# The first group of a feed-forward layer as plain products, and the block forms of x for two pairs at once

## The chip, the core and the metric

One core of a Trainium2 chip runs the whole program. The time is that of one execution on the device, in microseconds; the median of several runs is given. The engines run side by side, each with its own queue in program order: TensorE (PE), VectorE (DVE), ScalarE (ACT), GpSimd (POOL), and SyncE (SP), which issues most transfers. POOL issues the transfers that add to what lies in SBUF already.

## The reference

One layer on 512 tokens with 1024 features, in float32. The change touches the first line inside the loop:

```python
h = h + 0.5 * swiglu(rmsnorm(h, ffn1_norm[i]), ffn1_w_gate[i], ffn1_w_up[i], ffn1_w_down[i])
...
h = h + 0.5 * swiglu(rmsnorm(h, ffn2_norm[i]), ffn2_w_gate[i], ffn2_w_up[i], ffn2_w_down[i])
gate = jax.nn.sigmoid(rmsnorm(h, ple_norm[i]) @ ple_w_gate[i] + ple_b_gate[i])
h = h + gate * (p[i] @ ple_w_proj[i])
...
def swiglu(x, w_gate, w_up, w_down):
    return (jax.nn.silu(x @ w_gate) * (x @ w_up)) @ w_down
```

The hidden width of a feed-forward is 2816. Between the two stand a token mixer and its projections, which the change leaves alone.

## The kernel before

Features lie on the 128 partitions, tokens along the free side: `h[0..7]` are eight tiles of 128 x 512. Every product is done in three passes of a short format: an operand is split into a high part (a cast, ScalarE) and a low part (the difference, VectorE), and the passes are high by high, high by low and low by high (`whi`, `wlo` for weights; `Parts.split`, L422 and L423). The gain of the norm is applied to x first, the factor per token only behind the product, so the products need not wait for the norm.

A feed-forward works in 11 groups of 256 hidden columns. For a group, gate and up together are a 2 x 2 block product: the rows of blocks are up and gate, the inner blocks are the lower and upper four feature tiles, and the columns are the first and second 256 tokens. `Group` computes the four results with seven block products in place of eight (numbers 1 to 7), from sums of weight blocks and from block forms of x. With X11, X12 the two token halves of a tile of the first four and X21, X22 those of its partner four tiles on (a pair), the forms are X11, X2 (both halves), T3 = X22 - X12, T2 = X11 - T3, T4 = X21 - T2 and T1 = X11 - X12. They lie split in `xfa` and `xfb`, one of each per pair. Weight sums are made by accumulating transfers of POOL (L594, L606, L645) and by one addition on VectorE (L589). A block product is 24 matmuls with 256 columns (four pairs, two column blocks, three passes). `mm`, `acc` and `sm` are the tags of eight PSUM banks. Product 1 goes to an `mm` bank; `seed` copies it into an `acc` bank (L665), which products 6, 5 and 3 add to, while product 2 adds to the `mm` bank itself. A matmul of no use opens the `acc` bank in the first two groups (L653). `keep_p7` and `keep_u2` copy other partial results out.

The norm of the first feed-forward is formed beside the products: ScalarE squares the tiles of h, VectorE adds the squares (`ssum`, L266), TensorE sums them over partitions (L275), VectorE forms the inverse root, TensorE spreads it to all partitions (L305), ScalarE keeps it (`rall`, L311). Only then can gates be scaled and put through Silu.

The program starts with the embedding: two steps of 24 matmuls of 512 columns (L214 to L216), whose results ScalarE copies out (L832) and POOL stores to DRAM (L792). Then come, in the first feed-forward, products of group 0 and of group 1 mixed: (0,1), (1,1), (0,2), (0,7), (0,6), (1,2), (0,5), (0,4), (0,3), where (group, product) names a step; then (1,7), (1,6), (1,4), (1,5), (1,3) with two steps of the down projection between them. `run` writes all engines' queues from this list: the split of a step's weights stands two steps ahead of its product, its loads six, its `after` work one or two behind, and `also` and `ahead` hang further work on a step's split. Queues are strictly in that order. Split weights rotate through three buffers, a second pair (`whix`, `wlox`) serves steps that are named so.

In the first feed-forward, the block forms are made by `XForms.all_of` from h itself, scaled by the gain as they are split:

```python
also(steps[1], "split", blocks("X11", "X12"))
ahead(steps[3], "split", blocks("X2"))
ahead(steps[4], "split", blocks(("T3", 0)))
```

In the second one, `first` and `second` form them tile by tile as h becomes ready.

## Time and profile before

| | us |
|---|---|
| median of 3 runs (lowest, highest) | 1132.74 (1131.59, 1134.9) |
| the profiled execution | 1130.95 |
| its span, first to last instruction | 1129.2 |
| TensorE busy | 1085.7 (96%) |
| VectorE busy | 800.6 (71%) |
| ScalarE busy | 503.4 (45%) |

Mean granted TensorE clock 0.989. A row of the timeline reads: start, duration, engine, source line, operation, written tile <- read tiles, shape, count, and in brackets how long the engine had been idle and what ended that. A row of the chain has start, length, engine, tile, line. A row of a stretch has its bounds and length, then busy time and count of PE, PEld (weight loads), VectorE, ScalarE, POOL, and the granted clock, the share of the DMA engines and GB/s. Matmuls overlap in their records, so the pace is read from start to start and not from a duration.

### The profile page before, as it was taken

What the parts mean: (1) busy time and instruction counts of PE and PEld (TensorE: products, weight loads), DVE (VectorE), ACT (ScalarE), POOL (GpSimd) and SP (SyncE); (2) the same over time, 40 slices, a digit from 0 to 9 for tenths busy, and PEclk for the clock granted to TensorE, in tenths of its full rate; (3) what the DMA queues carried; (4) which work ended last, traced back from release to release, by engine and by line L of the source; (5) the groups of instructions that cost most, each with busy time, mean ns of one, the idle gap of its engine ahead of it and who ended that gap; (6) DMA issues with size and microseconds to landing.
All of it is one profiled execution on the core that took longest, in us unless ns stands there. A gap on an engine that the chain in (4) does not pass through costs nothing.

```text
span 1129.2 us, 16802 instructions
## 1 busy us (share of the span) xinstructions
PE 1085.7 (96%) x6781; PEld 963.6 (85%) x6781; DVE 800.6 (71%) x1099; ACT 503.4 (45%) x671; POOL 177.1 (16%) x161
## 2 busy tenths in 40 slices
PE   9589999999999999999999999998999999999997
PEld 7488999999998788777778888887999999999887
DVE  5767766766776687799875565767876676767766
ACT  6544444344344365423543343534444344344554
POOL 2000000000000301476421100010100000000312
PEclk9799999999999999999999999999999999999999
DMA  9667756666733222354333233588766667553412
GB/s 358 148 171 190 223 144 177 169 178 186 195 94 103 72 85 90 96 175 122 112 93 94 75 93 114 148 201 208 191 186 184 174 163 189 155 141 96 148 57 75
DMA packets 50190, 165.87 MB, mean 147 GB/s; under 512 B 5697, under 2 KB 5953, under 8 KB 50113
## 3 DMA queue, kind: packets, MB, share of 16 engines
q1 hardware_dynamic: 34416, 118.50, 30.9%
q0 software_dynamic: 10096, 36.70, 18.3%
q10 hardware_dynamic: 5600, 9.60, 2.8%
q8 instruction: 53, 0.87, 0.3%
q14 instruction: 25, 0.20, 0.1%
HBM read 160.52 MB, written 4.26 MB: 146 GB/s over the span
## 4 chain that ended last, share of the span: by engine, by line
PE 75%; DVE 11%; DMA 5%; ACT 4%; issue 3%; POOL 2%; DVEq 0%; ACTq 0%; POOLq 0%
PE mm L579 17%; PE acc L579 13%; PE sm L215 7%; PE sm L216 7%; PE sm L214 7%; PE mm L214 4%; PE mm L216 4%; PE mm L215 4%; PE acc L214 3%; PE acc L216 3%; PE acc L215 3%; DMA s<-in_ffn_gu 2%; DVE wlo L423 1%; ACT whi L422 1%; DMA u<-cs_dram 1%
## 5 line engine op out<-in xcount | busy, mean ns | idle before, releaser
L579 PE MATMUL mm<-xfb,whi 128*128 128x256 f32 x992 | 175.8, 280 | 12.4 <-ACT p L669 5.9
L579 PEld LDWEIGHTS mm<-xfb,whi 128*128 128x128 f32 x992 | 153.4, 191 | 15.2 <-ACT p L669 6.3
L423 DVE TENSOR_TENSOR wlo<-raw,whi 128x1024 fp32r<-128x1024 f32 x95 | 116.3, 1225 | 70.2 <-ACT whi L422 68.9
L422 ACT CAST whi<-raw 128x1024 fp32r<-128x1024 f32 x95 | 99.3, 1046 | 97.9 <-issue 38.9
L579 PE MATMUL mm<-xfb,wlo 128*128 128x256 f32 x496 | 138.8, 280 | 1.4 <-DVE wlo L423 1.4
L579 PE MATMUL acc<-xfb,whi 128*128 128x256 f32 x704 | 122.5, 276 | 1.8 <-ACT whi L422 1.1
L216 PE MATMUL sm<-ghi,wlox 128*128 128x512 f32 x296 | 116.5, 393 | 1.2 <-DVE wlox L423 1.2
L214 PE MATMUL sm<-ghi,whix 128*128 128x512 f32 x296 | 115.4, 390 | 0.7 <-ACT whix L422 0.7
L215 PE MATMUL sm<-glo,whix 128*128 128x512 f32 x296 | 115.9, 391 | 0.0
L579 PEld LDWEIGHTS acc<-xfb,whi 128*128 128x128 f32 x704 | 107.5, 188 | 3.9 <-ACT whi L422 1.2
L579 PE MATMUL acc<-xfb,wlo 128*128 128x256 f32 x352 | 97.5, 277 | 2.2 <-DVE wlo L423 2.2
L579 PEld LDWEIGHTS mm<-xfb,wlo 128*128 128x128 f32 x496 | 94.5, 190 | 2.1 <-DVE wlo L423 2.1
L423 DVE TENSOR_TENSOR wlox<-rawd,whix 128x1024 fp32r<-128x1024 f32 (+1 forms) x40 | 45.7, 1142 | 57.4 <-ACT whix L422 57.4
L689 ACT ACTIVATE g<-g 128x512 f32<-128x512 f32 x44 | 27.8, 632 | 121.0 <-DVE g L688 121.0
L594 POOL DMA_DIRECT2D raw<-in_ffn_gu x22 | 18.9, 858 | 389.4 <-DVE h L742 158.8
L184 ACT CAST whi<-raw 128x1024 fp32r<-128x1024 f32 x44 | 45.8, 1044 | 61.1 <-PE mm L215 22.7
L423 DVE TENSOR_TENSOR wlo<-rawb,whi 128x1024 fp32r<-128x1024 f32 x48 | 58.7, 1223 | 19.3 <-ACT whi L422 19.3
L742 DVE SCALAR_TENSOR_TENSOR h<-sm,h 128x512 f32<-128x512 f32 x96 | 63.4, 685 | 10.8 <-PE sm L216 10.2
L185 DVE TENSOR_TENSOR wlo<-raw,whi 128x1024 fp32r<-128x1024 f32 x44 | 57.5, 1308 | 18.9 <-ACT whi L184 13.8
L579 PEld LDWEIGHTS acc<-xfb,wlo 128*128 128x128 f32 x352 | 66.1, 188 | 2.8 <-DVE wlo L423 2.8
L216 PEld LDWEIGHTS sm<-ghi,wlox 128*128 128x128 f32 x296 | 55.5, 188 | 13.7 <-DVE wlox L423 2.1
L214 PEld LDWEIGHTS sm<-ghi,whix 128*128 128x128 f32 x296 | 55.6, 188 | 11.8 <-ACT whix L422 1.1
(366 smaller groups left out, 2644.9 us busy)
## 6 DMA issues: line engine op xcount, KB each, us to landing
raw<-in_ffn_gu SPq DMA_DIRECT2D x56, 512.0 KB, 5.9
rawd<-in_ffn_down SPq DMA_DIRECT2D x40, 512.0 KB, 4.1
raw<-in_ffn_gu POOLq DMA_DIRECT2D x34, 512.0 KB, 5.6
rawb<-in_ffn_gu SPq DMA_DIRECT2D x32, 512.0 KB, 5.4
raw<-in_w_in SPq DMA_DIRECT2D x29, 512.0 KB, 3.6
s<-in_ffn_gu SPq DMA_DIRECT2D x22, 512.0 KB, 7.1
s<-in_ffn_gu POOLq DMA_DIRECT2D x22, 512.0 KB, 8.5
raw<-in_w_out SPq DMA_DIRECT2D x16, 512.0 KB, 3.7
```

What stands on the lines that cost most here:

```text
L184: nc.scalar.copy(self.hi[:, c], self.raw[:, c])
L185: nc.vector.tensor_tensor(self.lo[:, c], self.raw[:, c], self.hi[:, c].bitcast(F32), ALU.subtract)
L214: nc.tensor.matmul(ps, whi, xhi, start=first, stop=False)
L215: nc.tensor.matmul(ps, whi, xlo, start=False, stop=False)
L216: nc.tensor.matmul(ps, wlo, xhi, start=False, stop=last)
L422: nc.scalar.copy(self.hi[:, :n], raw[:, :n])
L423: nc.vector.tensor_tensor(self.lo[:, :n], raw[:, :n], self.hi[:, :n].bitcast(F32), ALU.subtract)
L579: nc.tensor.matmul(o, wt[:, c], xt, start=fresh and p == m == n == 0, stop=last and n == 2, skip_group_check=True,)
L594: nc.gpsimd.dma_start(w21.raw, self.src[0], accum_op=ALU.add)
L689: nc.scalar.activation(t, t, AF.Silu)
L742: nc.vector.scalar_tensor_tensor(h[d], ps[d], 0.5, h[d], ALU.mult, ALU.add)
```

## The change

Group 0 of the first feed-forward is no longer seven block products but four plain steps: gate with the first four feature tiles, up with them, then gate and up with the other four. Each step is two chains, one per 128 output columns, of 12 matmuls with all 512 tokens: eight chains of 512 tokens in all. They need only X11, X12, X21 and X22, and the four weight blocks as they are, without sums. Group 1 follows whole, as (1,1), (1,7), (1,2), (1,6), (1,4), (1,5), (1,3). Its forms come from a copy of h that ScalarE scales by the gain once (`Early.x`), and each form is made for two pairs in one instruction (`Early.t`); `xfa` and `xfb` now hold two pairs each. The squares stand with the splits of steps 4 and 5 in place of 6 and 7, ahead of T3, T2, T4 and T1. The sums for the norm follow the second plain step, and the spread uses their bank. `plain_gate` scales and gates group 0 as soon as the norm is kept, `plain_finish` multiplies by up. One padding of 480 bytes goes. The second feed-forward keeps its steps.

```diff
-    "D1": 1, "X12": 1, "F": 1, "xfa": 4, "xfb": 4, "x": 16, "xs": 8, "u": 8, "emb": 8, "raw0": 1, "embt": 1, "rawb": 3,
+    "D1": 1, "X12": 1, "F": 1, "xfa": 2, "xfb": 2, "x": 16, "xs": 8, "u": 8, "emb": 8, "raw0": 1, "embt": 1, "rawb": 3,
-PAD = {"sb": 480, "ffn_left": 96, "mix_left": 160, "ple_left": 160, "ffn_right": 0, "mix_right": 96, "ple_right": 0}
+PAD = {"sb": 0, "ffn_left": 96, "mix_left": 160, "ple_left": 160, "ffn_right": 0, "mix_right": 96, "ple_right": 0}
-        def spread(diag):
-            ps = sm_ps()
+        def spread(diag, ps=None):
+            ps = sm_ps() if ps is None else ps
             nc.tensor.matmul(ps, ones, diag, start=True, stop=True)
-                got["ps"] = self.spread(got["diags"])
+                got["ps"] = self.spread(got["diags"], got["ps"])
+        def __init__(self, xfs):
+            if len(xfs) % 2:
+                self.both_a, self.both_b = xfs[-1].both_a, xfs[-1].both_b
+            else:
+                self.both_a = sb("xfa", (P, 2, 2, 2, HT), F32R)
+                self.both_b = sb("xfb", (P, 5, 2, 2, HT), F32R)
+            self.a, self.b = (t[:, :, :, len(xfs) % 2] for t in (self.both_a, self.both_b))
+            xfs.append(self)
-        @staticmethod
-        def all_of(xfs, what, stage=None):
...
+    class Early:
+        def __init__(self, a, b, d, name):
+            self.a, self.b, self.d, self.name = a, b, d, name
+            self.hg = [None, None]
+        def x(self, lower):
+            self.hg[lower] = sb(("ghi", "glo")[lower], (P, 2, T))
+            to = (self.a, self.b)[lower][:, 0:2]
+            for k in range(2):
+                d = self.d + k + NP * lower
+                nc.scalar.activation(self.hg[lower][:, k], h[d], AF.Copy, scale=col(self.name, d))
+            t = self.hg[lower].rearrange("p k (s t) -> p s k t", s=2)
+            nc.scalar.copy(to[:, :, 0], t)
+            nc.vector.tensor_tensor(to[:, :, 1], t, to[:, :, 0].bitcast(F32), ALU.subtract)
+        def t(self, i):
+            x11, x12, x21, x22 = (
+                t.rearrange("p k (s t) -> p s k t", s=2)[:, s] for t in self.hg for s in range(2)
+            )
+            if i == 3:
+                self.f = sb(("ghi", "glo")[self.d // 2], (P, 2, 2, HT))
+            n = (3, 2, 4, 1).index(i) % 2
+            f, other = self.f[:, n], self.f[:, 1 - n]
+            if i in (3, 1):
+                nc.vector.tensor_tensor(f, *((x22, x12) if i == 3 else (x11, x12)), ALU.subtract)
+            else:
+                nc.vector.scalar_tensor_tensor(
+                    f, x11 if i == 2 else x21, -1.0, other, ALU.mult, ALU.subtract
+                )
+            to = self.a[:, 1] if i == 1 else self.b[:, {3: 2, 2: 3, 4: 4}[i]]
+            nc.scalar.copy(to[:, 0], f)
+            nc.vector.tensor_tensor(to[:, 1], f, to[:, 0].bitcast(F32), ALU.subtract)
-            self.first, self.leads, self.last = j < 2, j == 0, j == sum(G_PARTS) - 1
-
-            self.other_pair = (1, 2, 7) if j == 1 else ()
+            self.first = j in ((1, 2) if plain else (0, 1))
+            self.early = j == 1 if plain else j < 2
+            self.leads, self.last = j == 0, j == sum(G_PARTS) - 1
+            self.other_pair = (1, 2, 7) if j == 1 and not plain else ()
-            early = self.first
+            early = self.early
+        def plain_steps(self):
+            self.g = sb("g", (P, 2, 2, HT))
+            self.ps = {}
+            def step(w, i, which, lower):
+                w_parts = {}
+                def split():
+                    w_parts[0] = w.split()
+                def product():
+                    whi, wlo = w_parts[0]
+                    if not lower:
+                        self.ps[which] = (
+                            [sm_ps(), sm_ps()] if which == "gate" else [bank("mm", 3), bank("acc", 2)]
+                        )
+                    for m, ps in enumerate(self.ps[which]):
+                        for p, xf in enumerate(self.xfs):
+                            c = slice((2 * p + m) * P, (2 * p + m + 1) * P)
+                            t = (xf.a, xf.b)[lower]
+                            passes(
+                                by_half(ps), whi[:, c], wlo[:, c], t[:, 0:2, 0], t[:, 0:2, 1],
+                                not lower and p == 0, lower and p == len(self.xfs) - 1,
+                            )
+                return Step(product, lambda: self.load((w, i)), None, split)
+            return [
+                step(*s) for s in (
+                    (self.w21, 2, "gate", False), (self.w11, 0, "up", False), (self.w22, 3, "gate", True), (self.w12, 1, "up", True),
+                )
+            ]
+        def plain_gate(self):
+            for m, ps in enumerate(self.ps["gate"]):
+                t = self.g[:, :, m]
+                nc.vector.tensor_tensor(t, by_half(ps), by_half(self.shared["r"]), ALU.mult)
+                nc.scalar.activation(t, t, AF.Silu)
+        def plain_finish(self):
+            for m, ps in enumerate(self.ps["up"]):
+                t = self.g[:, :, m]
+                nc.vector.tensor_tensor(t, t, by_half(self.shared["r"]), ALU.mult)
+                nc.vector.tensor_tensor(t, t, by_half(ps), ALU.mult)
-            if half == 0 or self.hi is None:
+            if half or self.last:
+                self.parts_of_g(slice(half, half + 1) if self.last else slice(0, 2))
+        def parts_of_g(self, part):
+            if self.hi is None:
                 self.hi = sb("ghi", (P, 2, 2, HT), F32R)
                 self.lo = sb("glo", (P, 2, 2, HT), F32R)
-            if half == 0 and not self.last:
-                return
-            part = slice(half, half + 1) if self.last else slice(0, 2)
-    def swiglu(name, xfs, norm, closed, after, at=2):
+    def swiglu(name, xfs, norm, closed, after, plain):
-        groups = [Group(src[j], xfs, shared, j) for j in range(sum(G_PARTS))]
-        gs = [g.steps() for g in groups]
+        groups = [Group(src[j], xfs, shared, j, plain) for j in range(sum(G_PARTS))]
+        gs = [None if plain and g.leads else g.steps() for g in groups]
-        steps = [gs[j][i] for j, i in ((0, 1), (1, 1), (0, 2), (0, 7), (0, 6), (1, 2), (0, 5), (0, 4), (0, 3))]
+        if plain:
+            steps = groups[0].plain_steps()
+        else:
+            steps = [gs[j][i] for j, i in ((0, 1), (1, 1), (0, 2), (0, 7), (0, 6), (1, 2), (0, 5), (0, 4), (0, 3))]
-                    for i in (7, 6, 4, 5, 3) if j == 1 else (1, 7, 6, 4, 5, 2, 3):
+                    for i in ((1, 7, 2, 6, 4, 5, 3) if plain else (7, 6, 4, 5, 3)) if j == 1 else (1, 7, 6, 4, 5, 2, 3):
-        norm.behind(steps[at:], D, lambda r: shared.update(r=r))
+        def use(r):
+            shared.update(r=r)
+            if plain:
+                groups[0].plain_gate()
+        norm.behind(steps[0 if plain else 2 :], D, use)
+        if plain:
+            also(gs[1][1], "after", groups[0].plain_finish)
+            also(gs[1][7], "after", lambda: groups[0].parts_of_g(slice(0, 2)))
-                ps.append(bank("mm", 3) if q == 0 and i < 3 else sm_ps() if i else bank("acc", 2))
+                ps.append(bank("acc", 2) if i == 3 else bank("mm", 3) if q else sm_ps())
-        splitter("mix_norm", x_mix), 3,
+        splitter("mix_norm", x_mix), True,
+        XForms(x_ffn1)
+    early = [Early(x_ffn1[d].both_a, x_ffn1[d].both_b, d, "ffn1_norm") for d in (0, 2)]
-    also(steps[2], "load", lambda: load_x(4, 5, 6, 7))
-
-    also(steps[1], "split", blocks("X11", "X12"))
-    ahead(steps[3], "split", blocks("X2"))
-    ahead(steps[4], "split", blocks(("T3", 0)))
-    ahead(steps[5], "split", blocks(("T3", 1)))
-    ahead(steps[6], "split", blocks(("T2", 0)))
-    also(steps[6], "split", blocks(("T2", 1)))
-    also(steps[7], "split", blocks("T1"))
-    also(steps[8], "split", blocks("T4"))
-    for k in range(2):
-        also(steps[6 + k], "split", lambda k=k: [norm.add(h[d]) for d in range(4 * k, 4 * k + 4)])
-    also(steps[6], "split", store_embedding)
+    also(steps[3], "load", lambda: load_x(4, 5, 6, 7))
+    also(steps[1], "split", lambda: [e.x(0) for e in early])
+    also(steps[3], "split", lambda: [e.x(1) for e in early])
+    also(steps[4], "split", lambda: squares(0, 1, 2, 3))
+    also(steps[5], "split", lambda: squares(4, 5, 6, 7))
+    also(steps[4], "split", store_embedding)
+    for k, i in enumerate((3, 2, 4, 1)):
+        also(steps[6 + k], "split", lambda i=i: [e.t(i) for e in early])
```

TensorE's queue at the sums for the norm, before (`acc_263` is product 6 of group 0, `mm_307` product 2 of group 1):

```order
L579 MATMUL acc_263<-xfb_250,whi_375 128x256 x2
L579 MATMUL acc_263<-xfb_250,wlo_376 128x256
L275 MATMUL sm_491<-ones_78,ssum_388 128x1 x4
L579 MATMUL mm_307<-xfb_247,whix_437 128x256 x2
L579 MATMUL mm_307<-xfb_247,wlox_438 128x256
```

And now (`acc_311` is up with the first four tiles, `sm_257` gate, which the other four tiles add to):

```order
L215 MATMUL acc_311<-xfa_113,whi_241 128x512
L216 MATMUL acc_311<-xfa_113,whi_241 128x512
L217 MATMUL acc_311<-xfa_113,wlo_242 128x512
L276 MATMUL sm_352<-ones_78,ssum_294 128x1 x4
L215 MATMUL sm_257<-xfb_112,whi_290 128x512
```

The sums moved from behind five products of 256 columns to behind two plain steps, ahead of the other two.

ScalarE's queue around a seed, before (`acc_263<-mm_265` is the seed of group 0, `acc_305<-mm_307` that of group 1):

```order
L422 CAST whi_301<-rawb_133 128x1024
L665 COPY acc_263<-mm_265 128x512
L504 CAST xfb_247<-ghi_166 128x256
L504 CAST xfb_248<-glo_168 128x256
L504 CAST xfb_249<-ghi_170 128x256
L504 CAST xfb_250<-glo_172 128x256
L422 CAST whi_341<-raw_135 128x1024
L665 COPY acc_305<-mm_307 128x512
```

And now around the seed of group 1 (`acc_447<-mm_449`; the casts into `xfb` from `ghi_385` and `glo_389` are T4, `g_109` the gates of group 0, `whi_523` the weights of product 6):

```order
L423 CAST whi_474<-rawb_255 128x1024
L527 CAST xfb_112<-ghi_385 128x512
L527 CAST xfb_114<-glo_389 128x512
L312 COPY rall_485<-sm_352 128x512
L712 ACT_TABLE_LOAD
L712 ACTIVATE g_109<-g_109 128x2x256 x2
L721 COPY acc_447<-mm_449 128x512
L423 CAST whi_523<-rawb_165 128x1024
```

The seed has moved behind T4, the kept norm, the load of the Silu table and both gates of group 0.

VectorE's queue, before, where T2 is formed and split behind product 6's weights and the additions of squares follow:

```order
L589 TENSOR_TENSOR raw_23_125<-raw_23_125,s_41_174 128x1024
L497 SCALAR_TENSOR_TENSOR ghi_166<-h_101,negffn_norm_111,ghi_166 128x256
L497 SCALAR_TENSOR_TENSOR glo_168<-h_102,negffn_norm_111,glo_168 128x256
L497 SCALAR_TENSOR_TENSOR ghi_170<-h_103,negffn_norm_111,ghi_170 128x256
L497 SCALAR_TENSOR_TENSOR glo_172<-h_104,negffn_norm_111,glo_172 128x256
L423 TENSOR_TENSOR wlo_376<-raw_23_125,whi_375 128x1024
L511 TENSOR_TENSOR xfb_247<-ghi_166,xfb_247 128x256
L511 TENSOR_TENSOR xfb_248<-glo_168,xfb_248 128x256
L511 TENSOR_TENSOR xfb_249<-ghi_170,xfb_249 128x256
L511 TENSOR_TENSOR xfb_250<-glo_172,xfb_250 128x256
L266 TENSOR_TENSOR ssum_388<-ssum_388,tmp_390 128x512
```

And now, from the diagonals of the norm to the first gate of group 0 (T2 and then T4, for two pairs each):

```order
L295 TENSOR_TENSOR tmp_408<-ident_72,rtok_393 128x512
L424 TENSOR_TENSOR wlo_437<-raw_199,whi_436 128x1024
L523 SCALAR_TENSOR_TENSOR ghi_385<-ghi_155,ghi_385 128x512
L528 TENSOR_TENSOR xfb_112<-ghi_385,xfb_112 128x512
L523 SCALAR_TENSOR_TENSOR glo_389<-ghi_160,glo_389 128x512
L528 TENSOR_TENSOR xfb_114<-glo_389,xfb_114 128x512
L424 TENSOR_TENSOR wlo_475<-rawb_255,whi_474 128x1024
L523 SCALAR_TENSOR_TENSOR ghi_385<-glo_245,ghi_385 128x512
L528 TENSOR_TENSOR xfb_112<-ghi_385,xfb_112 128x512
L523 SCALAR_TENSOR_TENSOR glo_389<-glo_250,glo_389 128x512
L528 TENSOR_TENSOR xfb_114<-glo_389,xfb_114 128x512
```

The forms moved behind the additions of squares and the norm, and a form's difference is followed at once by its own low part, with a cast of ScalarE between the two.

60 lines of the change are left out of this document (8 added, 52 removed).

## The prediction

> **What bounds the kernel now.** I read the page's busy times first, then the table of stretches, then TensorE's own timeline with what ended each gap.
>
> ```profile
> PE 1085.7 (96%) x6781; PEld 963.6 (85%) x6781; DVE 800.6 (71%) x1099; ACT 503.4 (45%) x671; POOL 177.1 (16%) x161
> ...
> 20.00:60.00 40.00, 25.95 (x178) 24.54 (x178) 29.15 (x61) 20.51 (x40) 6.07 (x8) 0.83 0.65 188
> 60.00:100.00 40.00, 35.31 (x248) 32.52 (x247) 27.71 (x34) 17.37 (x23) 4.28 (x5) 0.96 0.76 207
> 100.00:200.00 100.00, 99.57 (x724) 93.40 (x725) 72.37 (x82) 43.01 (x52) 8.52 (x10) 1.00 0.69 182
> ```
>
> TensorE is busy 96% of the span and full from 100 us on. Columns after the length are PE, PEld, DVE, ACT, POOL, then granted clock, DMA share and GB/s. The loss sits in 20 to 80 us, the place of the change: 14 us without a matmul in 20 to 60, at a mean clock of 0.83.
>
> ```profile
> 33.10 0.80 PE L579 MATMUL mm<-xfb,whi 128*128 128x256 f32 x2 [5.48 <-ACT whi L422]
> 34.36 0.58 PE L579 MATMUL mm<-xfb,wlo 128*128 128x256 f32 x1 [0.46 <-DVE wlo L423]
> 39.22 0.38 PE L579 MATMUL acc<-xfb,whi 128*128 128x256 f32 x1 [0.73 <-DVE xfb L511]
> 49.47 1.86 PE L275 MATMUL sm<-ones,ssum 128*128 128x1 f32 x8 [7.38 <-DVE ssum L266]
> 73.39 0.50 PE L579 MATMUL mm<-xfb,whi 128*128 128x256 f32 x2 [2.96 <-ACT p L669]
> 74.35 0.39 PE L579 MATMUL mm<-xfb,wlo 128*128 128x256 f32 x1 [0.46 <-DVE wlo L423]
> ...
> 33.00:36.70 3.70, 3.13 (x13) 2.84 (x14) 3.04 (x4) 1.09 (x3) 0.07 (x1) 0.50 1.06 260
> 51.20:54.20 3.00, 3.00 (x15) 3.00 (x16) 2.86 (x12) 3.00 (x7) 0.00 (x0) 0.51 0.00 0
> 73.30:77.90 4.60, 4.05 (x19) 3.85 (x20) 2.82 (x3) 2.50 (x5) 0.00 (x0) 0.64 0.30 81
> 740.00:744.00 4.00, 3.03 (x24) 2.83 (x25) 3.57 (x10) 2.54 (x4) 0.86 (x1) 1.00 1.07 241
> ```
>
> Brackets hold the idle time and its releaser. The first wait is for the summed weights of product 7, the second for the sum of squares behind all block forms on VectorE; together with 2.96 and the short ones 17.5 us. After each of the three long waits the granted clock is 0.50 to 0.64 for some 3 to 4 us; around 741 us, with waits near 1 us, it stays 1.00.
>
> **The matmuls.** Paces:
>
> ```profile
> 11.58 0.39 PE L214 MATMUL sm<-ghi,whi 128*128 128x512 f32 x1
> ...
> 18.58 0.39 PE L653 MATMUL acc<-whi 128*128 128x512 f32 x1
> ...
> 51.34 4.26 PE mm L579 x24
> ...
> 74.35 4.39 PE mm L579 x22
> 103.21 2.72 PE mm L579 x24
> ```
>
> Thirty matmuls of 512 start between the first two rows: 0.233 us each. A product of 24 by 256 takes 2.72 us (0.113 each), or 4.26 from a lowered clock. Removed: 7 products, 168 x 0.113 = 19.0. Added: 4 steps of 24, 96 x 0.233 = 22.4. So TensorE gets 3.4 us more work; any gain must come out of the 17.5 us of waits and the slow stretches, which cost 1.5 (4.26 - 2.72), 1.9 (4.39 - 22 x 0.113) and about 1.6 us (3.7 us at half clock less its waits). The matmuls that open a bank for the seed stay two in number.
>
> **The new schedule, step by step**, in the clock of the profile before. Durations:
>
> ```profile
> 45.48 2.21 ACT L265 ACTIVATE tmp<-h 128x512 f32<-128x512 f32 x4
> 52.96 1.99 ACT L422 CAST whi<-raw 128x1024 fp32r<-128x1024 f32 x2
> 60.88 1.28 ACT L689 ACT_TABLE_LOAD   x1
> 63.89 0.63 ACT L689 ACTIVATE g<-g 128x512 f32<-128x512 f32 x1 [1.73 <-DVE g L688]
> 73.23 0.62 ACT L422 CAST whi<-rawd 128x512 fp32r<-128x512 f32 x1
> ...
> 8.07 1.05 ACT L422 CAST whi<-raw 128x1024 fp32r<-128x1024 f32 x1
> 13.74 1.54 ACT L832 COPY rawd<-mm 128x512 f32<-128x512 f32 x3
> 32.01 1.04 ACT L422 CAST whi<-raw 128x1024 fp32r<-128x1024 f32 x1 [8.22 <-DMA raw<-in_ffn_gu]
> 32.96 0.58 ACT L665 COPY acc<-mm 128x512 f32<-128x512 f32 x1
> ...
> 46.34 3.08 DVE L266 TENSOR_TENSOR ssum<-ssum,tmp 128x512 f32<-128x512 f32 x4
> 53.40 0.15 DVE L232 TENSOR_SCALAR nv<-sm 128x4 f32<-128x4 f32 x1
> 55.64 0.69 DVE L294 TENSOR_TENSOR tmp<-ident,rtok 128x512 f32<-128x512 f32 x1
> 56.25 2.35 DVE L423 TENSOR_TENSOR wlo<-raw,whi 128x1024 fp32r<-128x1024 f32 x2
> 58.52 0.68 DVE L683 TENSOR_TENSOR g<-acc,p 128x512 f32<-128x512 f32 x1
> ```
>
> So ScalarE takes 0.53 us a 512 scaling or square, 0.95 a 1024 cast (1.05 to its end), 0.48 a copy, 0.62 a 512 cast; VectorE 1.14 a 1024 difference in a stream, 0.60 to 0.69 a 512 one, 0.80 each dependent addition.
>
> 1. Both embedding steps end at 18.58 as before. ScalarE has, from 9.0 us on (the cast of 8.07), two pairs of scalings with a wide cast (2.1 + 1.05), then the cast of gate-upper; VectorE ends that low part near 15.5, so the first plain step starts without a wait. Two steps: 18.6 + 48 x 0.233 = 29.8. The second waits for nothing: its weights are split by 18.4.
> 2. The sum of squares comes next on TensorE, ahead of the lower steps. ScalarE: 8 copies, two more pairs (up to 21.5), copies to 23.3, the cast of gate-lower 24.3, 4 squares, cast of up-lower 27.4, 4 squares. VectorE: 24.4 + 1.14 (low part of gate-lower) + 3 x 0.80 + 1.14 + 4 x 0.79 = 32.2. TensorE waits 32.2 - 29.8 = 2.4 us: what is left of the 7.38. The eight squares stand earlier because the T forms no longer precede them.
> 3. Sums 1.86, lower steps 48 x 0.233 = 11.2. Is the clock lowered by 2.4 us without work? The nearest rows are 2.96 (lowered) and 1.07 (not); 2.96 is nearer, so I add 1.6. The lower steps end at 46.9. The other end, full clock and sums in 1.5, is 44.9. [...]
> 4. The spread 0.55, seeding matmul 0.23, product 1 and product 7 of the second group 2.72 each: 53.1. Product 7 needs the block T3 (37 us), and its summed weights. That accumulating transfer stands on POOL behind the third embedding store, as before:
>
> ```profile
> 15.65 2.57 ACT L506 ACTIVATE xfb<-h,vec 128x512 fp32r<-128x512 f32 x4
> ...
> 20.43 0.53 POOL L792 DMA_DIRECT2D emb_dram<-embt  x1 [3.80 <-ACT embt L832]
> 20.95 0.91 POOL L594 DMA_DIRECT2D raw<-in_ffn_gu  x1
> ```
>
>    Issued at 20.95 it let ScalarE go at 32.0: 11.1 us. The store now waits for a copy that ends at 22.3, so it lands near 34; ScalarE asks for it only when the lower gate step frees the buffer of the split weights, after 39. On SP one weight load more stands ahead of x tiles 4 to 7; ScalarE comes to them at 17.1, where before it took them at 15.65 without a wait. The four plain blocks need no sums, and the second group's loads follow them. Cost zero, with 5 us of cover in front of the cast; without it each us late is a us lost.
> 5. **The new wait.** Product 2 adds to the bank that product 1 filled, and the seed, a ScalarE copy, must read it first. The second feed-forward pays that wait already:
>
> ```profile
> 732.60 0.51 PE L579 MATMUL mm<-xfb,whi 128*128 128x256 f32 x2 [1.03 <-ACT acc L665]
> 740.21 0.50 PE L579 MATMUL acc<-xfb,whi 128*128 128x256 f32 x2 [1.07 <-ACT whi L422]
> 741.47 0.38 PE L579 MATMUL acc<-xfb,wlo 128*128 128x256 f32 x1 [0.76 <-DVE wlo L423]
> ```
>
>    The seed now stands on ScalarE behind the T4 casts, the copy of the norm, the table load and both Silus. From 46.9: cast 1.1 (its buffer is freed by the last plain step), VectorE 1.14, T4 of both pairs (difference 0.68, cast 0.62, difference 0.60, with semaphores 1.96 a pair, the second pair's cast ending 1.3 in) to 52.4, norm copy 0.58, table load 1.28, gate product 0.69 and 0.60, Silu 0.63, seed 0.58: 56.7. TensorE waits 3.6 us, clock lowered (nearest row 2.96): product 2 ends at 56.7 + 4.26 = 61.0, product 6 at 63.7 (its low weights are there at 59.5).
> 6. VectorE is the bound of this stage. Behind the Silus: four finishing products 2.8, low weights of product 6 1.14, T1 of both pairs 2 x 1.96 = 3.9: 63.4. ScalarE behind the last T1 cast (62.7): copy of product 7 0.58, cast of g 0.95, cast of w22 1.05, to 65.2. VectorE then makes low g and low w22: 65.45 + 1.23 = 66.7. Product 4 thus waits 1.5 and about 1.2 us, near the two rows at 740 us, so at full clock.
> 7. The row to compare with is 74.35, the same low weights of w22. 74.35 - 66.7 = 7.65 earlier; the 22 matmuls behind it at full clock save another 1.9. From there both programs have the same order on every engine: 9.5 us gained and kept, since TensorE is full after 100 us, and the small waits there keep their places.
>
> Block forms in all: 40 VectorE and 28 ScalarE instructions, mostly of 256, become 20 and 20 of 512 or 1024; their sum is inside steps 1 to 6. The 2 x 256 strided operands of the wide casts are taken at the 1024 price; were they slower by 0.3 us each, step 2 would move by 1.2 at most. The eight plain chains read their moving operand as two pieces of 256; I take 0.233, since neither two matmuls of 256 (0.227) nor one of 512 is dearer. The padding's change moves addresses, no instruction, and is costed at nothing: no wait shown above is a wait for an address.
>
> **Sum.** The profiled execution took 1130.95, 1.8 below the median 1132.74 (within the noise of 0.3%, about 3.4 us, that a measurement of this kernel has). 1130.95 - 9.5 = 1121.5; against the median 1123.2, which I give.
>
> **Rivals.**
> - The 2.4 us gap leaves the clock full: steps 3 to 6 move 2.0 us earlier, 1121.2. For it: 1.07 kept the clock. [...] Chance 0.27 against 0.42 for the forecast.
> - Product 2 does not wait for the seed and VectorE hides: TensorE is dense after 46.9, product 4 at 58.5, 14.9 us before 73.39, and 1.9 more: 1115.9. Against it stands the row at 732.60. Chance 0.06.
> - Part of it is lost: the accumulated weights land late, or forms and casts are slower than their plain-layout rows. The row from 33.0 to 36.7 has a DMA share of 1.06, so late landings are possible: every us by which w21 lands after 48 us delays product 7. Gains of 2 to 7 us, 1126 to 1131, chance 0.15, a third of it within 0.3%.
> - Slower: a moving operand in two strided pieces streams more slowly. 96 matmuls share the cost, so it decides at 9.5 / 96 = 0.10 us each, at 0.33 in place of 0.233. If each piece cost what a 256 matmul costs on the mean of the slow row (4.26 / 24 = 0.178), a chain matmul would be 0.355 and the time 1132.7 - 9.5 + 96 x 0.122 = 1134.9. No row of before has such an operand. Chance 0.05.
> - Something not seen, of either sign: 0.05.
>
> Faster by over 0.3%: 0.42 + 0.27 + 0.06 + 0.10, 0.85; within 0.09; slower 0.06. The range takes the dense rival's neighbourhood and most of the losses: 1117 to 1130; the forecast's own is 1120 to 1126.
>
> **What would show it.** Right: the rows of 5.48 and 7.38 are gone, one wait of 2 to 3 us ends at the sum of squares near 32 us, the second group's product 2 waits some 3.5 us for a ScalarE copy into acc, product 4 starts near 65 us, and the distance from there to the end is that of before less 1.9. Wrong: 512-column matmuls over 0.25 us apart, product 7 waiting for a DMA, no wait at the seed, or new gaps after 80 us that give the time back.

## The result and the profile after

The changed kernel takes 1124.76 us (median of 4 runs, 1123.3 to 1126.32) where the kernel before takes 1133.05 (4 runs, 1131.59 to 1134.9): 8.3 us less, a ratio of 0.9926 with a 95% interval of 0.9906 to 0.9946. The forecast was 1123.2. The profiled execution took 1124.72, with a span of 1123.0.

The first view is a row of the changed kernel's table of stretches (length, PE, PEld, DVE, ACT, POOL, granted clock, DMA share, GB/s), the counterpart of the row of 20 to 60 us shown of before.

```profile
20.00:60.00 40.00, 34.61 (x186) 29.46 (x186) 30.48 (x49) 21.97 (x33) 6.01 (x8) 0.96 0.72 216
```

TensorE works 34.6 us of 20 to 60 at a mean clock of 0.96, where it was 26.0 at 0.83. Its timeline shows which waits are left: the first and the last matmul of the upper plain steps, then every row behind a wait up to product 4.

```profile
18.44 0.39 PE L215 MATMUL sm<-xfa,whi 128*128 128x512 f32 x1
29.40 0.40 PE L217 MATMUL acc<-xfa,wlo 128*128 128x512 f32 x1
32.13 1.05 PE L276 MATMUL sm<-ones,ssum 128*128 128x1 f32 x8 [2.33 <-DVE ssum L267]
54.10 0.51 PE L589 MATMUL mm<-xfb,whi 128*128 128x256 f32 x2 [3.06 <-ACT acc L721]
62.53 0.50 PE L589 MATMUL mm<-xfb,whi 128*128 128x256 f32 x2 [1.09 <-ACT whi L423]
63.98 0.39 PE L589 MATMUL mm<-xfb,wlo 128*128 128x256 f32 x1 [0.95 <-DVE wlo L424]
```

The waits of 5.48 and 7.38 are gone. The sum of squares still costs 2.33, product 2 waits 3.06 for the seed, product 4 waits 1.09 and 0.95. The row at 63.98, which stood at 74.35, is 10.4 us earlier; by the start of the mixer (371.78, before 383.76) it is 12.0. But these two executions differ by 6.2 at the end. Three waits of before and the same three of the changed kernel show where:

```profile
547.47 1.10 PE L305 MATMUL sm<-tmp,ones 128*128 128x512 f32 x2 [0.46 <-DVE tmp L294]
740.21 0.50 PE L579 MATMUL acc<-xfb,whi 128*128 128x256 f32 x2 [1.07 <-ACT whi L422]
765.12 0.50 PE L579 MATMUL mm<-xfb,whi 128*128 128x256 f32 x2 [2.91 <-ACT p L669]
```

```profile
536.14 1.55 PE L306 MATMUL sm<-tmp,ones 128*128 128x512 f32 x2 [2.28 <-DVE tmp L295]
730.84 0.51 PE L589 MATMUL acc<-xfb,whi 128*128 128x256 f32 x2 [1.42 <-ACT whi L423]
757.20 0.50 PE L589 MATMUL mm<-xfb,whi 128*128 128x256 f32 x2 [2.09 <-ACT p L725]
...
533.24:536.66 3.42, 1.14 (x5) 0.49 (x4) 3.18 (x7) 2.08 (x3) 1.27 (x1) 1.00 0.00 0
536.66:540.07 3.41, 3.41 (x9) 2.31 (x8) 3.33 (x5) 1.49 (x3) 0.24 (x1) 0.50 0.55 179
727.80:731.22 3.42, 2.00 (x18) 1.83 (x16) 1.62 (x2) 1.47 (x2) 0.00 (x0) 1.00 1.05 240
731.22:734.63 3.41, 2.66 (x14) 2.53 (x13) 3.17 (x10) 1.95 (x3) 0.86 (x1) 0.50 1.05 230
734.63:738.05 3.42, 3.42 (x18) 3.42 (x18) 2.32 (x6) 0.79 (x2) 0.00 (x0) 0.50 1.06 228
755.11:758.52 3.41, 0.86 (x5) 0.66 (x6) 2.77 (x3) 3.41 (x6) 0.00 (x0) 1.00 0.84 162
758.52:761.94 3.42, 3.42 (x19) 3.42 (x18) 1.42 (x2) 1.09 (x2) 0.00 (x0) 0.50 0.26 81
```

The instruction order there is the same in both programs, yet the gain falls from 11.3 us (547.47 against 536.14) to 9.4 and 7.9. Behind each wait of the changed kernel stand 3.4 or 6.8 us at a granted clock of 0.50. In such a stretch matmuls of 256 columns stand 0.213 us apart (55.54 to 58.74 of the changed kernel, 15 intervals) in place of 0.113, so a full 3.41 us costs 3.41 x (1 - 0.113 / 0.213) = 1.6 us of dense work. Between 100 and 1100 us before has one such stretch of 3.4 us (518.3 to 521.7), the changed kernel four, two of them in a row.

### The profile page after: what moved, and what is told of

Read it like the earlier page. It is cut to its first block, busy times and chain, and to the rows that moved or that the text cites. A ratio compares the mean times of both kernels' runs of the same rounds, so it can differ in the third digit from the quotient of the medians.

```text
span 1123.0 us, 16606 instructions
## 1 busy us (share of the span) xinstructions
PE 1088.7 (97%) x6709; PEld 962.9 (86%) x6709; DVE 793.6 (71%) x1072; ACT 502.0 (45%) x657; POOL 174.7 (16%) x158
## 4 chain that ended last, share of the span: by engine, by line
PE 78%; DVE 10%; ACT 4%; issue 3%; DMA 2%; POOL 1%; ACTq 0%; SPq 0%; DVEq 0%; POOLq 0%
PE mm L589 18%; PE acc L589 14%; PE sm L216 7%; PE sm L217 7%; PE sm L215 7%; PE mm L215 4%; PE mm L217 4%; PE mm L216 4%; PE acc L215 3%; PE acc L217 3%; PE acc L216 3%; DVE wlo L424 1%; DMA s<-in_ffn_gu 1%; ACT whi L423 1%; DMA u<-cs_dram 1%
## 5 line engine op out<-in xcount | busy, mean ns | idle before, releaser
L589 PE MATMUL mm<-xfb,whi 128*128 128x256 f32 x976 | 172.4, 279 | 7.3 <-ACT acc L721 4.1
L589 PEld LDWEIGHTS mm<-xfb,whi 128*128 128x128 f32 x976 | 150.5, 190 | 9.6 <-ACT acc L721 4.5
L589 PE MATMUL mm<-xfb,wlo 128*128 128x256 f32 x488 | 136.5, 280 | 1.4 <-DVE wlo L424 1.4
L589 PE MATMUL acc<-xfb,whi 128*128 128x256 f32 x672 | 118.8, 279 | 1.4 <-ACT whi L423 1.4
L589 PEld LDWEIGHTS acc<-xfb,whi 128*128 128x128 f32 x672 | 104.6, 191 | 3.3 <-ACT whi L423 1.5
L589 PE MATMUL acc<-xfb,wlo 128*128 128x256 f32 x336 | 94.3, 281 | 2.2 <-DVE wlo L424 2.2
L424 DVE TENSOR_TENSOR wlo<-rawb,whi 128x1024 fp32r<-128x1024 f32 x50 | 61.2, 1223 | 18.5 <-ACT whi L423 18.2
L185 ACT CAST whi<-raw 128x1024 fp32r<-128x1024 f32 x44 | 45.8, 1044 | 59.8 <-PE mm L216 22.6
L217 PEld LDWEIGHTS sm<-ghi,wlox 128*128 128x128 f32 x296 | 55.5, 188 | 13.7 <-DVE wlox L424 2.1
```

Source lines behind the costliest of these rows:

```text
L185: nc.scalar.copy(self.hi[:, c], self.raw[:, c])
L217: nc.tensor.matmul(ps, wlo, xhi, start=False, stop=last)
L424: nc.vector.tensor_tensor(self.lo[:, :n], raw[:, :n], self.hi[:, :n].bitcast(F32), ALU.subtract)
L589: nc.tensor.matmul(o, wt[:, c], xt, start=fresh and p == m == n == 0, stop=last and n == 2, skip_group_check=True,)
```

## The experiments

Two questions: what bounds the stage up to product 4 (row "low w22", the difference on VectorE that product 4 waits for), and where the gain of 12.0 goes later. The matmul of product 4 that reads low w22 starts 1.27 us behind it (62.71 and 63.98 in the changed kernel); the 63.8 in two of the expectations is this matmul. Each kernel is the changed one with the edit shown; times are medians, ratios are to the kernel before.

**A shift of the program.** If the place of the waits in time decides, moving all behind 91 us should move the losses.

```diff
+    def more():
+        ps = sm_ps()
+        for _ in range(26):        # the second kernel: 52
+            nc.tensor.matmul(ps.rearrange("p (c t) -> p c t", c=NC), ones_r,
+                             ones_r.unsqueeze(1).to_broadcast([P, NC, P]), start=True, stop=True)
+    also(steps[14], "after", more)
```

> The changed kernel with 26 more matmuls of 512 columns (26 x 0.233 = 6.1 us) on TensorE near 91 us, in its dense part; nothing reads their bank. Every wait behind them falls 6.1 us later. Theory P (the 5.8 us given back after 500 us are stretches of lowered clock whose place depends on the time at which the same short waits fall): the loss changes with the shift, so the time is anywhere from 1125 to 1131 and not 1130.9. Rival S (the later loss belongs to the changed program, wherever it falls): 1124.8 + 6.1 = 1130.9, with the wait of 2.28 at the spread of the mixer and lowered clock at 736 to 742 and 762 to 768.

> The same with 52 such matmuls, 12.1 us: everything behind 91 us stands within 0.1 us of where the kernel before has it. Theory P: the losses behind 500 us vanish, the time is that of before's profiled run, about 1131, and the granted clock in 738 to 772 is 1.00 as in before. Rival S: 1124.8 + 12.1 = 1136.9, with the lowered stretches shifted by 12.

Measured: 1129.2 (0.996, 0.9946 to 0.9974) and 1133.86 (1.0007, 0.9993 to 1.002). The added matmuls also swallow two waits of 0.61 and 0.71 that the changed kernel has near 85 and 88 us, so S is 1129.6 and 1135.6. The first time fits S and lies in P's range too, the second lies between S and P's 1131. The lowered stretches fit neither: with the longer shift a single window behind 100 us is lowered, from 743.7, where P had none and S four. The traces gave a third theory. In the first shifted kernel (the granted clock is the third figure from the end):

```profile
28.65:32.07 3.42, 0.69 (x3) 0.21 (x2) 3.11 (x5) 2.14 (x4) 0.00 (x0) 1.00 1.05 241
32.07:35.48 3.41, 3.22 (x12) 2.94 (x13) 2.73 (x5) 0.62 (x1) 0.00 (x0) 0.50 1.05 305
...
735.20:738.62 3.42, 2.34 (x20) 2.10 (x18) 1.70 (x2) 1.55 (x2) 0.00 (x0) 1.00 1.02 241
738.62:742.03 3.41, 2.66 (x13) 2.60 (x13) 3.13 (x11) 1.87 (x3) 0.86 (x1) 0.50 1.06 231
```

Its clock is lowered behind the sum of squares, where nothing was shifted, and where the changed kernel's own profile kept full clock:

```profile
28.08:31.49 3.41, 1.72 (x8) 1.05 (x6) 3.10 (x5) 2.58 (x4) 0.00 (x0) 1.00 1.07 249
31.49:34.91 3.42, 2.78 (x16) 2.47 (x17) 2.73 (x4) 0.62 (x1) 0.00 (x0) 1.00 1.05 272
```

The windows in these rows are not chosen by eye. In each profile the clock's edges (found in slices of 1 us) fall on one grid with a period of 3.413 us, within 0.013 us root mean square; between profiles the grid's offset against the program differs, 0.5 to 3.3 us. So theory R, a reading of these rows: at each grid point the clock is set for one window by how much of the window before it TensorE worked. The wait for the sum of squares, with the sums of one column behind it, lies almost whole in one window of the shifted kernel (0.69 us of work) and is cut in two in the other (1.72 and 2.78). Low w22 starts at 65.86 in the one and 62.71 in the other: 3.15 us between two executions, with the same program up to there.

This pair alone does not separate the place of a wait from its length, since the wait is 2.92 us in the shifted kernel and 2.33 in the other. Of the six profiles that have it, the four with a lowered window show 2.85 to 2.94, the two without 2.25 and 2.33. Rows shown above and further down do separate them. Before waits 2.91 us at 765.12 and keeps the clock, with the wait cut at 764.12 into windows with 1.50 and 1.95 us of work. The changed kernel waits 2.09 at 757.20, has 0.86 us of work in the window, and the next one is lowered.

**The kernel before once more.**

> The kernel before, unchanged, profiled a second time. Theory R (the granted clock changes only at times on a grid of 3.41 us, as every lowered stretch of the six profiles so far does, and where the grid lies against the program differs from execution to execution): the lowered stretches last 3.4 or 6.8 us again, but begin at other places than 30.2, 47.3, 74.6 and 518.3, and the wait at the mixer's spread is 0.46 or about 2.2 us according to whether one falls near 520. Rival P (the place of a wait in the program decides): the same stretches within 0.5 us.

This is one more execution, of 1131.97 us. Its edges again fall on a grid (offset 1.38, first profile 2.92). In the second profile:

```profile
519.02 0.50 PE L216 MATMUL mm<-x,wlo 128*128 128x512 f32 x1 [1.71 <-DVE wlo L185]
548.44 1.10 PE L305 MATMUL sm<-tmp,ones 128*128 128x512 f32 x2 [2.12 <-DVE tmp L294]
738.64:742.06 3.42, 1.96 (x16) 1.68 (x15) 2.25 (x3) 2.29 (x3) 0.00 (x0) 1.00 1.05 265
742.06:745.47 3.41, 3.35 (x15) 3.35 (x16) 2.96 (x14) 1.13 (x2) 0.86 (x1) 0.50 1.03 246
```

The stretch at 518 is gone, one at 742 has come, and the wait at the mixer's spread is 2.12 in place of 0.46. R holds, P falls: one program, two executions, other stretches. One of them, from 45.8 us behind the wait for the sum of squares, lasts three windows, 10.2 us, where 3.4 or 6.8 was expected. The scatter of the times fits R too: of 21 executions of the kernel before that were timed beside the first four kernels, the fastest (1131.16) had a mean clock of 0.987 and the slowest (1136.24) 0.981. R also offers a reason for the 0.46: the lowered stretch at 518.34 stands ahead of that wait and holds TensorE back, with matmuls of 512 columns 0.427 us apart there, while VectorE keeps its pace in lowered stretches (a 1024 difference takes 1.22 us at 55.65 of the changed kernel, in one, and 1.22 at 62.71, outside); the wait takes it up.

**What bounds the stage: the sum one step later.**

```diff
-        norm.behind(steps[0 if plain else 2 :], D, use)
+        norm.behind(steps[1 if plain else 2 :], D, use)
```

> The changed kernel with the sum of squares one step later on TensorE, behind the lower gate step. The 2.33 us wait for the sum goes, and the seed copy comes ahead of the norm's copy, table load and Silus on ScalarE, so the 3.06 us wait at product 2 falls to 2 or less. Theory V (VectorE, without an idle moment but its round trips to ScalarE from 31 to 64 us, sets when product 4 starts): low w22 still starts at 63.8 +- 0.4, the time saved comes back as a wait of about 4 us at product 6 for its low weights (56.8), and the time is 1124.8, within 1.0. Rival Q (each wait of TensorE costs its length): 3 to 5 us less, 1120 to 1122.

Measured 1123.14 (0.9906, 0.9889 to 0.9923). The wait of 2.33 is gone, that of 3.06 is 0.98, and low w22 starts where it did:

```profile
50.51 0.50 PE L589 MATMUL mm<-xfb,whi 128*128 128x256 f32 x2 [0.98 <-ACT acc L721]
54.68 0.50 PE L589 MATMUL acc<-xfb,whi 128*128 128x256 f32 x2 [1.16 <-ACT whi L423]
57.06 0.38 PE L589 MATMUL acc<-xfb,wlo 128*128 128x256 f32 x1 [1.88 <-DVE wlo L424]
...
62.84 1.22 DVE L424 TENSOR_TENSOR wlo<-raw,whi 128x1024 fp32r<-128x1024 f32 x1
```

The time saved came back as 3.0 us of waiting at product 6, and product 4's matmul starts at 64.11. V holds on these rows: when the two TensorE waits on which the prediction spent most words shrank, product 4 came no earlier. The median is 1.6 under the changed kernel's, outside V's 1.0 and above Q's 1122; the two intervals overlap, so part of it can be chance. A reason that R offers, not tested by itself: without the wait there is no lowered window behind the sums, which four of the six profiles with that wait show; low w22's matmul comes 1.9 to 3.2 us later in three of them (67.13 and 65.84 in the two shifted kernels, 66.18 in the one with the padding moved, whose matmuls are also slower, against 63.98).

**T forms interleaved.**

```diff
-        also(steps[6 + k], "split", lambda i=i: [e.t(i) for e in early])
+        also(steps[6 + k], "split", lambda i=i: ([e.t(i) for e in early],
+             [e.high() for e in early], [e.low() for e in early]))
```

(`t` makes the difference, `high` the cast, `low` the low part, each for one pair of tiles.)

> The changed kernel with the T forms of both pairs interleaved: difference, difference, cast, cast, low, low, in place of one pair behind the other, so VectorE does not wait 0.69 us for each cast. Theory V: T4 and T1 lie on VectorE's path behind 45.4, each saves 2 x 0.69 = 1.4 less what is left of the second round trip, so low w22 starts 2.6 us earlier, at 61.2, and 1122.2; T3 and T2 save nothing, since the casts behind them wait for TensorE's buffers. Rival Q (TensorE's waits set the time): low w22 at 63.8 less the seed's gain of 1.3, 1123.5.

Measured 1123.55 (0.9908, 0.9891 to 0.9925). T4, from its first difference to the next instruction of VectorE, in the changed kernel and interleaved:

```profile
46.52 0.68 DVE L523 SCALAR_TENSOR_TENSOR ghi<-glo,ghi 128x512 f32<-128x512 f32 x1
47.89 0.69 DVE L528 TENSOR_TENSOR xfb<-ghi,xfb 128x512 fp32r<-128x512 f32 x1 [0.69 <-ACT xfb L527]
...
50.48 1.22 DVE L599 TENSOR_TENSOR rawb<-rawb,s 128x1024 f32<-128x1024 f32 x1
```

```profile
49.57 0.68 DVE L523 SCALAR_TENSOR_TENSOR ghi<-glo,ghi 128x512 f32<-128x512 f32 x1
50.17 0.68 DVE L523 SCALAR_TENSOR_TENSOR glo<-glo,glo 128x512 f32<-128x512 f32 x1
...
52.16 1.22 DVE L605 TENSOR_TENSOR rawb<-rawb,s 128x1024 f32<-128x1024 f32 x1
...
63.00 1.22 DVE L424 TENSOR_TENSOR wlo<-raw,whi 128x1024 fp32r<-128x1024 f32 x1
```

3.96 us became 2.59. This profile has the lowered window behind the sums; against the first shifted kernel, which has it too, low w22 is 2.9 earlier (65.86 to 63.00), where V said 2.6 and Q 1.3. The time does not tell them apart: Q had 1123.5, and V's 1122.2 lies within the interval.

**Both edits.**

> Both edits together: sums one step later, T forms interleaved. Theory V (VectorE bounds the stage to product 4): low w22 at 60.2 (62.8 in the one, less the 2.6 of the other), and 2.6 us under the one with the sums later: 1120.5. Rival Q (TensorE's waits set the time): the two edits remove the same wait at product 2, so low w22 at 62.5 and 1123.

Measured 1118.4 (0.9871, 0.9849 to 0.9893), low w22 at 57.59: 5.1 before the changed kernel, not 2.5. V named the engine and missed the size. T3 and T2 count now too. In the interleaved kernel VectorE waits 4.04 us between T3 and T2 for a cast that itself waits until TensorE, held up by the sums and the lowered clock, frees its buffer; here it waits 0.25. So the place of the sums, worth nothing alone, counts once VectorE is faster. Q's 62.5 and 1123 are out.

**Two pairs at once, undone.** The interleaved kernel with each T form in pieces of 256, as before:

```diff
-            nc.vector.tensor_tensor(to[:, 1], f, to[:, 0].bitcast(F32), ALU.subtract)
+            for k in range(2):
+                nc.vector.tensor_tensor(to[:, 1, k], f[:, k], to[:, 0, k].bitcast(F32), ALU.subtract)
     ... the difference and the cast likewise
```

> The kernel with the T forms interleaved, but each form made in pieces of 256 columns as in the kernel before (twice the instructions: 8 differences and 8 low parts of 256 on VectorE for each two forms, in place of 4 and 4 of 512); this undoes 'two pairs at once' in the T forms. From the 256 rows of before (418 to 478 ns to the end, some 0.35 and 0.40 from start to start) T4 takes about 3.2 us on VectorE from its first difference to the next instruction: 0.6 more than interleaved (2.59), 0.8 less than in the changed kernel, where one pair stands behind the other (3.96). Theory V: low w22 at 64.0 where the window behind the sums is lowered, 61.2 where not; the time 1124.5, that is within 1.5 of both. Rival W (wide instructions are what the forms gain by): slower than the changed kernel by 8 x 4 x 0.06 = 2 us or more, 1127.

Measured 1120.94 (0.9888, 0.9874 to 0.9902), not above the kernel with 512 wide forms.

```profile
46.54 0.76 DVE L526 SCALAR_TENSOR_TENSOR ghi<-glo,ghi 128x256 f32<-128x256 f32 x2
...
49.22 1.23 DVE L608 TENSOR_TENSOR rawb<-rawb,s 128x1024 f32<-128x1024 f32 x1
...
60.01 1.22 DVE L424 TENSOR_TENSOR wlo<-raw,whi 128x1024 fp32r<-128x1024 f32 x1
```

T4 takes 2.68: 0.09 more than in wide pieces, and 1.28 less than in the changed kernel. V's figures, from 3.2 for T4, came out too late (low w22 61.2 and 1124.5). W is refuted: the T forms gained next to nothing by their width, and lost by one pair standing behind the other. (That this kernel is faster than the interleaved one fits its profile's full clock behind the sums, which is chance by R.)

**The clock's windows, filled.** Matmuls that nothing reads, set shorter than the wait they stand in:

```diff
+    def keep_busy(n, ps=None):
+        ps = sm_ps() if ps is None else ps
+        for _ in range(n):
+            nc.tensor.matmul(ps.rearrange("p (c t) -> p c t", c=NC), ones_r,
+                             ones_r.unsqueeze(1).to_broadcast([P, NC, P]), start=True, stop=True)
...
+            keep_busy(self.fill, ps)      # in Norm.sums: 8 for the first norm (on both edits 0)
...
+        if g:                             # in finish_group; in the second pair of kernels: if not g
+            keep_busy(8, ps)
...
+                if busy.get((self.plain, self.j, i)):     # in Group.product: 6, 4, 5, 8 (on both edits 0, 4, 5, 8)
+                    keep_busy(busy[self.plain, self.j, i])
```

> The changed kernel with matmuls that nothing reads put in front of six waits of TensorE, each set shorter than its wait: 8 before the sum of squares, 6 and 4 before products 2 and 4 of the second group, 8 before the spread of the mixer's second group, 5 before product 6 of the second feed-forward's first group, 8 before product 4 of its second. Theory R with 'a grid window with some 1.7 us or more without matmuls lowers the clock of the next': no lowered clock between 10 and 1100 us in any execution; the four lowered windows behind 500 us of the changed kernel's profile go (1.7 + 1.5 + 1.5 us, since waits behind two of them grow), and the window behind the sums, which two of its variants showed (3.1 us at low w22) and it did not, cannot come: about 1120, 1118 to 1122. Rival S (the waits cost their time whatever the clock does): 1124.8 within 1, or more where a filling outlasts its wait.

> Both edits, and matmuls that nothing reads in front of four waits (4 before product 4 of the second group, 8, 5 and 8 at the three places behind 500 us). Theories R and V: the gains add, 1120.5 - 4 = 1116.5, with no lowered clock behind 80 us until 1100. Rival S: 1120.5, as without the filling.

> The changed kernel with the six fillings, that of the mixer before its first group's spread. Theory R: 1.9 us under the first filled kernel, 1120.5, which is 4.3 under the changed kernel: what the lowered windows cost it on the mean of its executions. Rival S: 1122.4, as with the filling in the other place, since waits and not the clock cost the time.

> Both edits and the filling, with the eight matmuls for the mixer now before the spread of its first group, where the wait of 2.28 stands (before the second group's, where they stood, TensorE waited for nothing, and they added 8 x 0.233 = 1.9 us). Theory R: 1.9 us under the kernel with the filling in the wrong place, 1113.8, the wait at that spread 0.3 to 0.5, no lowered clock until 1100. Rival: the spread's sums wait for VectorE, whose chain TensorE's extra matmuls could delay; then 1115.7.

Measured: 1122.36 (0.9906, 0.9886 to 0.9926) and, on both edits, 1115.66 (0.9846, 0.9824 to 0.9868). R had 1118 to 1122 and 1116.5, S 1124.8 and 1120.5. The filling for the mixer stood before the wrong group's spread; put right, 1121.03 (0.9895, 0.9878 to 0.9912) and 1114.46 (0.983, 0.9817 to 0.9843). Here R had 1120.5 and 1113.8, the rivals 1122.4 and 1115.7: the intervals hold both, and it is the trace that decides. The same spread before and behind that correction, in the changed kernel with the fillings:

```profile
538.34 1.10 PE L316 MATMUL sm<-tmp,ones 128*128 128x512 f32 x2 [2.29 <-DVE tmp L305]
```

```profile
537.32 1.13 PE L316 MATMUL sm<-tmp,ones 128*128 128x512 f32 x2 [0.42 <-DVE tmp L305]
...
20.00:60.00 40.00, 37.28 (x211) 31.46 (x210) 30.62 (x49) 21.95 (x34) 6.02 (x8) 1.00 0.71 214
500.00:800.00 300.00, 292.44 (x1616) 249.77 (x1615) 206.84 (x310) 125.09 (x170) 58.07 (x46) 1.00 0.46 131
```

In this profile of the kernel with six fillings the clock is 1.00 from 20 to 1100 us. Its median is 3.7 us under the changed kernel's (expected 4.3), with no other work moved, though the two intervals just touch. That is about what lowered windows cost the changed kernel. Not every window went in every execution, though that had been expected: of the five of this kernel the three with a mean clock of 0.997 or 0.998 took 1119.59 to 1121.03, the two with 0.993 took 1123.43 and 1124.58. The first filled kernel's profile has 6.8 us of lowered clock from 63.1, the best kernel's 3.4 at 54.3 and at 501.4, each behind a wait of 1.7 to 1.9 us that is left there. The kernel with both edits and the corrected filling is the fastest here, 1114.46, 10.3 under the changed one.

**The padding.**

```diff
-PAD = {"sb": 0, "ffn_left": 96, ...
+PAD = {"sb": 480, "ffn_left": 96, ...
```

> The changed kernel with the padding of the static area back at 480. All theories: addresses move and nothing else, 1124.8 within 1.0, low w22 at 62.7 or 65.9.

Measured 1138.43 (1.0037, 1.0023 to 1.0052): 13.7 us over the changed kernel, and slower than before. All theories missed. The groups of 256-column matmuls in 110 to 360 us and two rows that span the dense stretch, first of the changed kernel, then with the padding back:

```profile
L589 PE MATMUL mm<-xfb,whi 128*128 128x256 f32 x370 | 64.1, 276 | 0.0
88.45 0.39 PE L589 MATMUL acc<-xfb,wlo 128*128 128x256 f32 x1 [0.71 <-DVE wlo L424]
371.78 0.50 PE L972 MATMUL mm<-x,whi 128*128 128x512 f32 x1 [0.75 <-DVE convin L980]
```

```profile
L589 PE MATMUL mm<-xfb,whi 128*128 128x256 f32 x384 | 69.0, 281 | 0.0
90.65 0.38 PE L589 MATMUL acc<-xfb,wlo 128*128 128x256 f32 x1 [0.75 <-DVE wlo L424]
379.78 0.50 PE L972 MATMUL mm<-x,whi 128*128 128x512 f32 x1 [0.72 <-DVE convin L980]
```

289.1 us in place of 283.3 for the same instructions with no other wait between: 5.8 us in the first feed-forward. The mean record of these matmuls is 281 ns in place of 276, and from start to start they stand 0.118 us apart in place of 0.113, while matmuls of 512 columns keep their 0.227. From the like of the first row in the second feed-forward to the last sums on TensorE, 791.87 to 1128.33, it is 336.5, where the first shifted kernel took 330.6: 5.8 again. Another 2.2 us are there at 90.65 already, against 88.45. In the kernel before, the dense stretch (100.43 to 383.76) took 283.3 as in the changed one. The change took out a table of 8 numbers per partition (32 bytes) and 480 of padding, 512 together, and the pace stayed; with 480 put back it does not. That the 32 bytes are what decides is a reading of the code: no run moved them alone.

## Why the prediction was right, and where it was not

1. *First plain steps without a wait, 18.6 to 29.8.* Right: 18.44, the last matmul starts at 29.40. (29.40 - 18.44) / 47 = 0.233 each, the 0.233 of before's one-piece rows, so the two-piece moving operand cost nothing here, and the rival that made the kernel slower had no effect to rest on.
2. *The sum of squares waits 2.4.* Right, 2.33 (2.25 to 2.94 in the six profiles that have this wait).
3. *Clock lowered behind it.* Here the step fails. In the changed kernel's profile the clock stayed up, and the spread behind the lower steps starts at 44.33 (44.9 forecast for full clock, 46.9 for the value taken). In four of six profiles with this wait it was lowered. I asked whether a gap of 2.4 is long enough, with neighbours of 2.96 and 1.07; the runs show that a gap's length alone does not decide (2.91 kept the clock, 2.09 lowered it), since its place on a grid of 3.413 us counts. Both ends were real, with odds between them. Nor were the windows ahead of half clock idle throughout: 0.69 us of work at 28.65 in the first shifted kernel, 1.71 at 514.93 of before.
4. *Product 7 does not wait for its weights.* Right: no wait for a DMA at TensorE from 18 to 64 us.
5. *The seed waits 3.6, with the clock lowered behind it.* Right in kind: 3.06, and one window is lowered. That the wait is harmless, because VectorE sets product 4, the prediction implied in step 6, and the sum one step later showed it.

```profile
51.97:55.38 3.41, 1.28 (x11) 1.28 (x12) 3.24 (x6) 2.69 (x4) 0.00 (x0) 1.00 0.02 5
55.38:58.80 3.42, 3.42 (x19) 3.42 (x18) 2.73 (x5) 0.62 (x1) 0.84 (x1) 0.50 0.05 5
```

6. *VectorE bounds, product 4 waits 1.5 and 1.2.* Right: 1.09 and 0.95. The matmul behind the second wait was forecast for 66.7, or 64.7 with full clock behind the sums. It came at 63.98, 0.7 early, and with the lowered window at 67.13 and 65.84 in the two shifted kernels, 0.4 late and 0.9 early.
7. *9.5 us gained and kept, "since TensorE is full after 100 us, and the small waits there keep their places".* The first half was too small for this profile (12.0 at 371.78, which includes the 1.6 for the stretch behind low w22), the second wrong: the waits kept their places, and still cost more. From product 4's low matmul to the end the forecast was before's distance less 1.9; it is before's plus 4.2 (1059.0 against 1054.9). Waits of 1 to 2.3 us were costed at their length; behind three of them (2.28, 1.42 and 2.09) stood four windows at half clock in this profile, up to 1.6 us each. 12.0 became 6.2 in this pair of executions, and 8.3 by the medians. So 9.5 was near by two errors of opposite sign, and that is luck.
8. *Padding at nothing.* Right for the change as a whole, by the pace that stayed, and wrong as a rule: I looked for a wait for an address, and the address shows in the pace: 0.118 us from start to start with the padding back, 0.113 without.

The block forms, whose fewer and wider instructions step 6 carried inside its sum, gained next to nothing by width where this was tried, in the T forms: the changed order cost VectorE 1.3 to 1.4 us a form, of which the prediction's 1.96 a pair already held the round trip.

What stays open: why the profiles of the changed kernel and its variants without filling, shift or moved padding show 2 to 4 lowered windows behind 100 us and both of before one. With offsets that differ by execution it can be chance; two profiles of before don't tell. Nor does a run separate the four plain steps from the earlier place of the squares, both of which stand behind the fall of the 7.38 to 2.33. And the threshold: a window with 1.9 us idle kept the clock (760.70 of before, at 1.50 us of work), one with 1.70 idle lowered it:

```profile
514.93:518.34 3.41, 1.71 (x11) 1.23 (x10) 3.41 (x5) 0.10 (x1) 2.70 (x2) 1.00 0.58 140
518.34:521.75 3.41, 3.41 (x9) 2.63 (x9) 2.82 (x4) 2.56 (x4) 1.95 (x2) 0.50 0.61 192
...
760.70:764.12 3.42, 1.50 (x14) 1.31 (x12) 2.21 (x4) 1.53 (x2) 0.89 (x2) 1.00 1.04 205
764.12:767.53 3.41, 1.95 (x14) 1.75 (x15) 2.99 (x4) 3.41 (x6) 0.00 (x0) 1.00 1.06 211
```

Counted over all fourteen profiles from 20 us on, with sums of one column left out of the work, the border is narrow. Every window at full clock with up to 1.45 us of work was followed by half clock, and none with 1.73 or more was. Between 1.52 and 1.71, ten were and fifteen were not, and what decides there is not known.

## What to carry to other kernels

Ask of each wait which engine ends it and whether that engine was itself idle: here two TensorE waits of 5.4 us together were worth nothing alone. Taking out the round trips of 0.69 us on VectorE, in eight places, brought low w22 forward by 2.9 us alone and by 5.2 with the sums moved as well (62.84 to 57.59). A wait of one to three microseconds on TensorE could cost its length here, and in some executions a window at half clock behind it as well, up to 1.6 us (behind 2.09 at 757.20 of the changed kernel, not behind 2.91 at 765.12 of before); forecast it as two cases with odds, and where it can't be removed, fill it with matmuls that nothing reads. Don't compare two profiled executions to explain a few microseconds before the lowered stretches of both are laid side by side, and keep the addresses fixed when only the program is to change: 480 bytes of padding made 13.7 us here.

## What the runs showed of the hardware that I had not expected

- In the fourteen profiles the granted clock changed on a grid of 3.413 us, which the executions met at different offsets (2.92 and 1.38 in the two of before). From 20 us on, every window at full clock with 1.45 us of work or less was followed by half clock, and none with 1.73 or more. A lowered window with 2.66 us of work (731.22) was followed by another; over the fourteen profiles this went up to 2.76, and from 2.93 on full clock followed.
- Matmuls of one column seem to count as idle: the window 735.20 to 738.62 of the first shifted kernel had 1.08 us without work and was followed by half clock, but 0.94 of its "busy" time were the eight sums. With such sums counted as work the border above disappears: a window with 2.34 us lowered the next, one with 1.50 did not. No run tested that alone.
- Matmuls of 256 columns ran some 4% slower (0.118 against 0.113 us from start to start), in both feed-forwards, with the static area 480 bytes further on, while those of 512 columns kept their 0.227; nothing in the waits shows it.
- Two VectorE instructions of 256 columns took little more than one of 512 in a stream: 0.67 us (46.54 to 47.21, the two differences of a pair, in pieces of 256) against 0.60 (49.57 to 50.17, interleaved in wide pieces).
